# Differential attention: scores of blocks 3 and 4 from stacked rounded and low key halves, and softmax sums folded into the head's norm factor

## The chip, the cores and the metric

The kernel runs on one core of a Trainium2 chip. The metric is device microseconds per execution, lower is better. The kernel as it stands takes 2959.73 us (median of three runs, 2958.84 to 2962.85).

## The reference, cut to what matters

Two layers, each a mixer and a PEER channel mixer, on 512 tokens of width 1024 in float32. The mixer of a layer concatenates three parts (differential attention, short gated convolution, gated linear attention, GLA for short), multiplies by `w_out` and adds to `x`. The change touches the first part alone:

```
def block(args):                       # one of four blocks of 128 queries
    s = jnp.einsum('bqhmd,bkhmd->bhmqk', qi, k).astype(jnp.float32) * scale
    mask = kpos[None, :] <= qpos[:, None]
    p = jax.nn.softmax(jnp.where(mask, s, -jnp.inf), axis=-1)
    a = p[:, :, 0] - lam * p[:, :, 1]
    return jnp.einsum('bhqk,bkhe->bqhe', a.astype(v.dtype), v)
...
o = rmsnorm(o, gain) * out_scale       # over the 128 values of a head
```

There are four heads, and each has two score maps (m = 0, 1) with 64 dimensions. Since the norm divides each head's row by its own size, a factor common to the whole row drops out of it, but for the small eps.

## The kernel before, in words

The 512 tokens are four blocks `tb` = 0 to 3 of 128 queries; "blocks 3 and 4" are `tb` = 2 and 3. `qT` and `kT` hold queries and keys with the head dimensions on partitions: map 0 of a head on rows 0 to 63, map 1 on rows 64 to 127. Block `tb` looks at `(tb + 1) * 128` keys.

A projection product is float32 split in two: `split` (L84, L85) rounds a tile to float32r on ScalarE (`hi`) and takes the rest on VectorE (`lo`); `mm3` (L79 to L81) makes hi·hi + hi·lo + lo·hi, three float32r matmuls. Scores don't use this. They are plain float32 matmuls (L486), and so that one map can be multiplied with 128 rows, `turned_queries` (L477) copies the queries into `qz`, whose rows of the other map are zero.

For each head, `head_weights` makes two scores (L486), adds the causal mask by a bfloat16 matmul (L487), takes the row maximum (L488 on VectorE), the exponentials with their row sums (L493 on ScalarE), and then on VectorE the reciprocals of both sums (L495), map 1's factor with lambda (L496), map 1 times that factor (L497), and the difference (L498). `diff_attention` transposes this on TensorE (`atr`, L512), copies it to SBUF on ScalarE (`aT`, L514) and multiplies it with the values (`po`, L516). `head_norm` squares the four heads of a block in one ScalarE instruction (`ho`, L524), sums on VectorE (`hss`, L525), takes the reciprocal root and multiplies (L527). `head_out` transposes (`htr`, L535) and splits into `mh` and `ml` (L536, L537).

The rest of the mixer is interleaved with this. After the GLA part come blocks 0 and 1, with slab products `psp` of `w_in` (columns from 2048, 1792 and 1536, the three factors of the convolution) between them. In the slab from 1536, after its first half, stand the weights of two heads of block 2 (`early`); `mch` and `mcl` are the convolution's result. Then `w_out` is loaded in eight chunks of 128 rows: `woraw` (SyncE's queue, two buffers in turn), `woh` (ScalarE cast, L84) and `wol` (VectorE, L85). Chunks come in the order `korder` = 6, 7, 4, 5, 0, 1, 2, 3. `out_proj` (`pso`) uses them in that order for both column halves of a block, so that the second pair of products can end only when chunk 3 is there. Two PSUM buffers hold `pso`, two hold `po`, `atr` and `htr`, four hold scores.

The instructions of each engine run in the order in which the building framework's scheduler put them: it keeps program order where data demands it, and otherwise interleaves by its own estimate of times. The placement of tiles in SBUF follows the pools: a pool that is closed gives its memory to the next one opened on that side, and the first writer of such a tile waits for the last readers of what lay there.

Of the kernel before, what the change touches and what calls it, by code (L numbers as in the profile page):

```python
# [7 lines left out]
F32 = mybir.dt.float32  # L8
F32R = mybir.dt.float32r
# [5 lines left out]
OP = mybir.AluOpType  # L15
# [48 lines left out]
def bc(ap, pattern):  # L64
    return bass.AP(tensor=ap.tensor, offset=ap.offset, ap=[ap.ap[0]] + pattern)


class K:
# [152 lines left out]
    def mixer(self, L):  # L221
# [3 lines left out]
        with ExitStack() as mc:  # L225
            mp = mc.enter_context(tc.tile_pool(name="mix", bufs=1, reuse_waits="tile"))
            dgain = mp.tile([P, 1], F32, name="dgain")
            cw = mp.tile([P, 2, 3], F32, name="cw")
            qT = mp.tile([P, 4, T], F32, name="qT")
            kT = mp.tile([P, 4, T], F32, name="kT")  # L230
            va = mp.tile([P, TB, T], F32, name="va")
            if L == 0:
# [5 lines left out]
            with ExitStack() as wc:  # L238
                wp = wc.enter_context(tc.tile_pool(name="wpool", bufs=2, reuse_waits="tile"))
# [75 lines left out]
                lam = mp.tile([P, 1], F32, name="lam")  # L315
                nc.vector.tensor_tensor(lam, le[:, 0:1], le[:, 1:2], op=OP.subtract)
                nc.vector.tensor_scalar(lam, lam, lam_init, None, op0=OP.add)
                nc.vector.tensor_scalar(dgain, dgain, 1.0 - lam_init, None, op0=OP.mult)
# [47 lines left out]
                ap = ac.enter_context(tc.tile_pool(name="attn", bufs=2, side="right", reuse_waits="tile"))  # L366
                qz = [ap.tile([P, 4, 2, P], F32, name=f"qz{i}", bufs=1) for i in range(2)]
                for t in qz:
                    nc.gpsimd.memset(t, 0.0)
                heads = []  # L370

                def attend(tb, early=()):
                    heads.append(self.diff_attention(tb, qT, kT, va, qz[tb % 2], lam, ap, early))

                attend(0)
# [17 lines left out]
                for j, ps in across(1536):  # L393
                    if j == 0:
                        self.turned_queries(2, qT, qz[0])
                        early = [self.head_weights(2, h, kT, qz[0], lam, ap) for h in range(2)]
                    nc.vector.tensor_tensor(ys[j], ys[j], ps, op=OP.mult)
                    self.split(mch[:, j], mcl[:, j], ys[j])

            with tc.tile_pool(name="wout", bufs=1, reuse_waits="tile") as op_:  # L400
# [31 lines left out]
                for tb in range(TB):  # L432
                    if tb > 1:
                        attend(tb, early if tb == 2 else ())
                    t = slice(tb * P, tb * P + P)
                    self.head_out(heads[tb], dgain, mh[:, 0:4, t], ml[:, 0:4, t])
# [35 lines left out]

    def turned_queries(self, tb, qT, qz):
        s = slice(tb * P, tb * P + P)
        for m in range(2):
            r = slice(64 * m, 64 * m + 64)
            self.nc.scalar.copy(qz[r, :, m], qT[r, :, s])  # L477

    def head_weights(self, tb, h, kT, qz, lam, ap):
        nc = self.nc  # L480
        nk = (tb + 1) * P
        st = self.sm.tile([P, 8], F32, tag="st", name="st")
        pss = []
        for m in range(2):
            ps = self.psA.tile([P, T], F32, tag="a", name="pss")
            nc.tensor.matmul(ps[:, 0:nk], qz[:, h, m], kT[:, h, 0:nk], start=True, stop=False)  # L486
            nc.tensor.matmul(ps[:, tb * P:nk], self.identb, self.causal, start=False, stop=True)  # L487
            nc.vector.tensor_reduce(st[:, m:m + 1], ps[:, 0:nk], axis=AX.X, op=OP.max)  # L488
            pss.append(ps)
        nc.vector.tensor_scalar(st[:, 2:4], st[:, 0:2], -0.125, None, op0=OP.mult)  # L490
        e = ap.tile([P, 2, T], F32, tag="e", name="e")
        for m in range(2):
            nc.scalar.activation(e[:, m, 0:nk], pss[m][:, 0:nk], AF.Exp, bias=st[:, 2 + m:3 + m],  # L493
                                 scale=0.125, accum_out=st[:, 4 + m:5 + m])
        nc.vector.reciprocal(st[:, 6:8], st[:, 4:6])  # L495
        nc.vector.tensor_tensor(st[:, 7:8], st[:, 7:8], lam, op=OP.mult)  # L496
        nc.vector.tensor_scalar(e[:, 1, 0:nk], e[:, 1, 0:nk], st[:, 7:8], None, op0=OP.mult)  # L497
# [4 lines left out]
    def diff_attention(self, tb, qT, kT, va, qz, lam, ap, early=()):  # L502
        nc = self.nc
        early = list(early)
        if not early:
            self.turned_queries(tb, qT, qz)
        po = self.psB.tile([P, 4, P], F32, tag="b", name="po")
        for h in range(4):
            e = early.pop(0) if early else self.head_weights(tb, h, kT, qz, lam, ap)
            tr = self.psB.tile([P, 4, P], F32, tag="b", name="atr")  # L510
            for kb in range(tb + 1):
                nc.tensor.transpose(tr[:, kb], e[:, 0, kb * P:kb * P + P], self.ident)  # L512
            aT = ap.tile([P, 4, P], F32, tag="aT", name="aT")
            nc.scalar.copy(aT[:, 0:tb + 1], tr[:, 0:tb + 1])  # L514
            for kb in range(tb + 1):
                nc.tensor.matmul(po[:, h], aT[:, kb], va[:, kb, h * P:h * P + P],  # L516
                                 start=(kb == 0), stop=(kb == tb))
        return self.head_norm(po, 4, P, ap)

    def head_norm(self, po, nh, hd, pool):  # L520
# [3 lines left out]
        nc.scalar.activation(o, po, AF.Square)  # L524
        nc.vector.tensor_reduce(ss, o, axis=AX.X, op=OP.add)  # L525
# [756 lines left out]
```

## Time and profile before

| what | value |
|---|---|
| median of three runs | 2959.73 us (2958.84 to 2962.85) |
| profiled execution, its own time | 2958.37 us |
| its span, first to last instruction | 2956.6 us |
| TensorE busy | 2925.6 us (99%) |
| VectorE busy | 2394.7 us (81%) |
| ScalarE busy | 1256.3 us (42%) |
| granted TensorE clock | 0.999 |
| score matmuls L486 (both layers) | 128 instructions, two for each score |

The stretch that the change touches is 146 to 240 us in the first layer, and the same stretch some 1467.7 us later in the second. In a timeline a row gives start, duration, engine, line, operation, output and inputs, partitions and elements, and the number of instructions merged. Matmuls are pipelined: one's duration is longer than its step, so the price of one is read as the distance between the starts of two. A float32 matmul stands as two instructions.

### The profile page before, as it was taken

To read this page: it belongs to the slowest core of one execution; us is meant where nothing else is said; L and a number is where in the kernel's file an instruction comes from. 1 tells how busy PE (TensorE), PEld (TensorE's weight loads), DVE (VectorE), ACT (ScalarE), POOL (GpSimd) and SP (SyncE) were. 2 spreads that over 40 slices of the span, in tenths; PEclk is the share of its full clock that TensorE was granted. 3 is DMA by queue.
4 is the path that set the end of the run, shared out by engine and by line. 5 is a ranking of instruction groups with operands and counts; after the bars stand their busy time and mean duration, and the time that the engine had idled before them with its cause. 6 is when DMAs were issued, how large, how long until landed. Compare 5 with 4: busy or idle time off the path is not lost.

```text
span 2956.6 us, 44538 instructions
## 1 busy us (share of the span) xinstructions
PE 2925.6 (99%) x16262; PEld 2606.0 (88%) x16262; DVE 2394.7 (81%) x4754; ACT 1256.3 (42%) x1860; POOL 716.0 (24%) x617
## 2 busy tenths in 40 slices
PE   8999999999999999999999999999999999999998
PEld 7878899999999999888888788999999999988887
DVE  6676999976887788877866769999768787888778
ACT  6253355665333332333453433556653333333333
POOL 1200000222444455222012000012225444452220
PEclk9999999999999999999999999999999999999999
DMA  4322257999999998999633222679999999989995
GB/s 130 92 72 77 93 172 250 321 301 362 348 338 326 330 346 310 368 333 342 251 96 90 67 82 86 205 253 330 303 351 356 333 337 332 332 316 358 346 347 203
DMA packets 335835, 760.24 MB, mean 257 GB/s; under 512 B 30688, under 2 KB 191360, under 8 KB 331520
## 3 DMA queue, kind: packets, MB, share of 16 engines
q1 hardware_dynamic: 160624, 435.19, 41.4%
q0 software_dynamic: 75776, 271.62, 26.0%
q10 hardware_dynamic: 99216, 50.60, 5.7%
q8 instruction: 127, 2.08, 0.3%
q14 instruction: 92, 0.75, 0.1%
HBM read 673.15 MB, written 81.00 MB: 255 GB/s over the span
## 4 chain that ended last, share of the span: by engine, by line
PE 84%; DVE 11%; ACT 2%; issue 2%; DMA 1%; SPq 0%; DVEq 0%; ACTq 0%
PE pv L80 11%; PE pv L81 11%; PE pv L79 11%; PE psh L79 9%; PE psh L81 9%; PE psh L80 9%; PE psp L80 2%; PE psp L81 2%; PE psp L79 2%; PE psq L80 2%; PE psq L79 2%; PE psq L81 2%; PE pss L486 1%; PE psg L1211 1%; PE pss L764 1%
## 5 line engine op out<-in xcount | busy, mean ns | idle before, releaser
L827 POOL DMA_INDIRECT row<-in_u_rows,idx x256 | 349.1, 1363 | 1337.6 <-DVE row L834 627.8
L80 PE MATMUL pv<-vl,wh 128*128 128x512 f32 x1500 | 583.9, 389 | 0.4 <-DVE vl L931 0.3
L81 PE MATMUL pv<-vh,wl 128*128 128x512 f32 x1500 | 583.4, 389 | 0.0
L79 PE MATMUL pv<-vh,wh 128*128 128x512 f32 x1500 | 583.2, 389 | 0.0
L827 POOL DMA_INDIRECT row<-in_v_rows,idx x256 | 315.7, 1233 | 597.0 <-DVE yacc L843 548.2
L745 ACT ACTIVATE ht<-psh 128x384 f32<-128x384 f32 x256 | 125.7, 491 | 742.1 <-PE psh L81 741.9
L931 DVE TENSOR_TENSOR vl<-vraw,vh 128x1024 fp32r<-128x1024 f32 x250 | 305.9, 1224 | 115.2 <-ACT vh L936 104.2
L79 PE MATMUL psh<-ahi,uwb 128*128 128x384 f32 x1024 | 346.9, 339 | 0.0
L79 PE MATMUL psh<-ahi,uwa 128*128 128x384 f32 x1024 | 346.4, 338 | 0.0
L81 PE MATMUL psh<-ahi,uwa 128*128 128x384 f32 x1024 | 344.6, 337 | 0.7 <-DVE uwa L730 0.7
L80 PE MATMUL psh<-alo,uwa 128*128 128x384 f32 x1024 | 344.3, 336 | 0.0
L80 PE MATMUL psh<-alo,uwb 128*128 128x384 f32 x1024 | 344.2, 336 | 0.0
L81 PE MATMUL psh<-ahi,uwb 128*128 128x384 f32 x1024 | 344.1, 336 | 0.0
L81 PEld LDWEIGHTS pv<-vh,wl 128*128 128x128 f32 x1500 | 281.4, 188 | 59.6 <-DVE wl L931 1.0
L80 PEld LDWEIGHTS pv<-vl,wh 128*128 128x128 f32 x1500 | 281.4, 188 | 56.6 <-DVE vl L931 2.2
L79 PEld LDWEIGHTS pv<-vh,wh 128*128 128x128 f32 x1500 | 281.6, 188 | 53.9
L843 DVE SCALAR_TENSOR_TENSOR yacc<-row,wk,yacc 128x1024 f32<-128x1024 f32 x254 | 325.2, 1280 | 1.7
L944 ACT CAST wh<-ht 128x384 fp32r<-128x384 f32 x250 | 127.9, 512 | 433.6 <-DVE ht L1096 417.0
L834 DVE SCALAR_TENSOR_TENSOR row<-row,xg 128x1024 f32<-128x1024 f32 x256 | 308.0, 1219 | 0.0
L730 DVE TENSOR_TENSOR uwa<-uraw,uwa 128x1024 fp32r<-128x1024 f32 x144 | 175.7, 1223 | 134.7 <-ACT uwa L729 134.5
L936 ACT CAST vh<-vraw 128x1024 fp32r<-128x1024 f32 x250 | 262.6, 1050 | 9.7 <-DMA vraw<-in_v_rows 9.7
L730 DVE TENSOR_TENSOR uwb<-uraw,uwb 128x1024 fp32r<-128x1024 f32 x144 | 175.8, 1222 | 105.9 <-ACT uwb L729 105.9
(361 smaller groups left out, 5708.6 us busy)
## 6 DMA issues: line engine op xcount, KB each, us to landing
uraw<-in_peer_u SPq DMA_DIRECT2D x256, 512.0 KB, 5.6
vraw<-in_v_rows SPq DMA_DIRECT2D x256, 512.0 KB, 6.5
G<-stg ACTq DMA_DIRECT2D x48, 1024.0 KB, 7.6
g<-G SPq DMA_DIRECT2D x32, 1536.0 KB, 10.0
H<-ht SPq DMA_DIRECT2D x144, 192.0 KB, 4.7
ht<-H SPq DMA_DIRECT2D x144, 192.0 KB, 6.5
wraw<-in_w_in SPq DMA_DIRECT2D x84, 256.0 KB, 3.2
uraw<-in_peer_w_q SPq DMA_DIRECT2D x32, 512.0 KB, 3.5
```

The lines of the kernel that those rows point to most:

```text
L79: mm(ps, ah, bh, start=first, stop=False)
L80: mm(ps, ah, bl, start=False, stop=False)
L81: mm(ps, al, bh, start=False, stop=last)
L486: nc.tensor.matmul(ps[:, 0:nk], qz[:, h, m], kT[:, h, 0:nk], start=True, stop=False)
L730: self.last = pin(nc.vector.tensor_tensor(lo, src, hi.bitcast(F32), op=OP.subtract))
L745: pin(nc.scalar.activation(hs[c], ps, AF.Gelu))
L827: nc.gpsimd.indirect_dma_start(out=r, out_offset=None, in_=ins[name], in_offset=bass.IndirectOffsetOnAxis(ap=idx[:, k:k + 1], axis=0))
L834: nc.vector.scalar_tensor_tensor(r, r, 1.0, xg, op0=OP.mult, op1=OP.mult, accum_out=hd[:, k:k + 1])
L843: nc.vector.scalar_tensor_tensor(yacc, r, wk[:, k:k + 1], yacc, op0=OP.mult, op1=OP.add)
L931: self.last = pin(nc.vector.tensor_tensor(lo, src, hi.bitcast(F32), op=OP.subtract))
L936: pin(nc.scalar.copy(vh[c], vs[c]))
L944: pin(nc.scalar.copy(wh[c], hs[c]))
```

## The change

Scores of blocks 2 and 3 are made from float32r halves. `ks[m]` holds the rounded keys of map m on that map's own 64 rows and their low parts on the other 64, brought there by a GpSimd DMA. `qa` holds the rounded queries of a map on both halves of the rows (the second copy by DMA too), `qb` the low queries. A score is then two float32r matmuls: `qa` with all 128 rows of `ks[m]` (hi·hi + hi·lo), and `qb` with the 64 rows of rounded keys (lo·hi). Keys are stacked block by block (`stack_keys`) behind the slab products, and queries of block 2 and 3 likewise (`stack_queries`); blocks 0 and 1 keep the padded float32 queries.

The weights of a head are no longer normalised by map 0's sum: map 1 is multiplied by -lambda times the ratio of the two sums and added to map 0, which leaves out the instruction on L497. Map 0's sums go into `s0`; `head_norm` takes their reciprocals, squares each head with that scale (four ScalarE instructions with row sums, in place of one and the VectorE sum on L525), and multiplies the norm's factor by it. `lam` changes its sign.

`qT` and `kT` move into a pool that closes with the slabs' pools, so that the first tiles of the `w_out` pool lie where they were.

```
+            raw_qk = wc.enter_context(tc.tile_pool(name="rawqk", bufs=1, reuse_waits="tile"))
+            qT = raw_qk.tile([P, 4, T], F32, name="qT")
+            kT = raw_qk.tile([P, 4, T], F32, name="kT")
...
+                ks = [ap.tile([P, 4, T], F32R, name=f"ks{i}", bufs=1) for i in range(2)]
+                kl = wc.enter_context(tc.tile_pool(name="klow", bufs=2, side="right", reuse_waits="tile"))
...
+                def stack_keys(tb):
+                    t = slice(tb * P, tb * P + P)
+                    lo = kl.tile([P, 4, P], F32R, tag="klo", name="klo")
+                    for m in range(2):
+                        r = half[m]
+                        self.split(ks[m][r, :, t], lo[r], kT[r, :, t])
+                        nc.gpsimd.dma_start(ks[m][half[1 - m], :, t], lo[r])
...
+                def stack_queries(tb):
+                    qa = ap.tile([P, 2, 4, P], F32R, tag="qa", name="qa")
+                    qb = ap.tile([P, 4, P], F32R, tag="qb", name="qb")
+                    for m in range(2):
+                        r = half[m]
+                        self.split(qa[r, m], qb[r], qT[r, :, tb * P:tb * P + P])
+                        nc.gpsimd.dma_start(qa[half[1 - m], m], qa[r, m])
+
+                    def stacked(ps, h, m, nk):
+                        nc.tensor.matmul(ps, qa[:, m, h], ks[m][:, h, 0:nk], start=True, stop=False)
+                        nc.tensor.matmul(ps, qb[half[m], h], ks[m][half[m], h, 0:nk], start=False, stop=False)
+                    return stacked
...
                 for j, ps in across(2048):
                     nc.scalar.copy(z[:, j, 2:], ps)
-                attend(1)
+                    stack_keys(j)
+                attend(1, padded_queries(1))
                 for j, ps in across(1792):
                     nc.vector.tensor_tensor(z[:, j, 2:], ps, z[:, j, 2:], op=OP.mult)
+                    if j:
+                        score2 = stack_queries(2)
+                    else:
+                        stack_keys(2)
...
                     if j == 0:
-                        self.turned_queries(2, qT, qz[0])
-                        early = [self.head_weights(2, h, kT, qz[0], lam, ap) for h in range(2)]
+                        s0 = self.sums()
+                        early = [s0] + [self.head_weights(2, h, score2, lam, ap, s0) for h in range(2)]
+                        stack_keys(3)
+                        score3 = stack_queries(3)
...
-            nc.tensor.matmul(ps[:, 0:nk], qz[:, h, m], kT[:, h, 0:nk], start=True, stop=False)
+            score(ps[:, 0:nk], h, m, nk)
...
-        nc.vector.reciprocal(st[:, 6:8], st[:, 4:6])
-        nc.vector.tensor_tensor(st[:, 7:8], st[:, 7:8], lam, op=OP.mult)
-        nc.vector.tensor_scalar(e[:, 1, 0:nk], e[:, 1, 0:nk], st[:, 7:8], None, op0=OP.mult)
-        nc.vector.scalar_tensor_tensor(e[:, 0, 0:nk], e[:, 0, 0:nk], st[:, 6:7], e[:, 1, 0:nk],
-                                       op0=OP.mult, op1=OP.subtract)
+        nc.vector.reciprocal(st[:, 4:5], st[:, 4:5])
+        nc.vector.scalar_tensor_tensor(st[:, 5:6], st[:, 4:5], lam, s0[:, h:h + 1], op0=OP.mult, op1=OP.mult)
+        nc.vector.scalar_tensor_tensor(e[:, 0, 0:nk], e[:, 1, 0:nk], st[:, 5:6], e[:, 0, 0:nk],
+                                       op0=OP.mult, op1=OP.add)
...
-        nc.scalar.activation(o, po, AF.Square)
-        nc.vector.tensor_reduce(ss, o, axis=AX.X, op=OP.add)
+        nc.vector.reciprocal(s0, s0)
+        for h in range(nh):
+            nc.scalar.activation(o[:, h], po[:, h], AF.Square, scale=s0[:, h:h + 1], accum_out=ss[:, h:h + 1])
         rstd = self.rsqrt(ss, hd)
+        nc.vector.tensor_tensor(rstd, rstd, s0, op=OP.mult)
         nc.vector.tensor_tensor(o, po, bc(rstd, [[1, nh], [0, hd]]), op=OP.mult)
```

ScalarE in block 0 of the first layer, before. `e` are exponentials, `qz` the padded queries, `aT` the transposed weights, `ho` the squares.

```order
L477 COPY qz_1504<-qT 64x4x128 x2
L84 CAST wh<-wraw 128x512
L493 ACTIVATE e,st<-pss,st 128x128 x4
L477 COPY qz_1503<-qT 64x4x128 x2
L514 COPY aT<-atr 128x128
L493 ACTIVATE e,st<-pss,st 128x128 x2
L379 COPY z<-psp 128x512
```

The same engine, the end of block 0 after the change (lines are the changed file's).

```order
L526 ACTIVATE e,st<-pss,st 128x128
L84 CAST ks_1506<-kT 64x4x128
L545 COPY aT<-atr 128x128
L84 CAST ks_1507<-kT 64x4x128
L84 CAST qa<-qT 64x512
L545 COPY aT<-atr 128x128
L84 CAST qa<-qT 64x512
L84 CAST ks_1506<-kT 64x4x128
L560 ACTIVATE ho,hss<-po,s_1517 128x128 x4
```

Casts of keys and queries now stand between the copies `aT` for which TensorE's `po` waits, and all casts of blocks 0 to 3 stand ahead of the slab from 1536.

TensorE where block 2's last heads give way to block 3's scores, before. `mgh` is GLA's result in `out_proj`.

```order
L512 MATMUL atr<-ident,e 128x128 x3
L486 MATMUL pss<-kT,qz_1504 128x512
L487 LDWEIGHTS identb
L487 MATMUL pss<-causal,identb 128x128
L486 MATMUL pss<-kT,qz_1504 128x512
L516 MATMUL po<-va,aT 128x128 x3
```

The same place after the change.

```order
L543 MATMUL atr<-ident,e 128x128 x3
L393 MATMUL pss<-ks_1506,qa 128x512
L394 MATMUL pss<-ks_1506,qb 128x512
L520 LDWEIGHTS identb
L520 MATMUL pss<-causal,identb 128x128
L393 MATMUL pss<-ks_1507,qa 128x512
L394 MATMUL pss<-ks_1507,qb 128x512
```

A score is two matmuls in place of one, of 128 and of 64 rows, with the mask behind them as before.

TensorE around the last chunk of `w_out`, before; the last row but one is the first that reads chunk 3.

```order
L535 MATMUL htr<-ident,ho 128x128 x4
L512 MATMUL atr<-ident,e 128x128 x4
L80 MATMUL pso<-wol,mh 128x512
L81 MATMUL pso<-woh,ml 128x512
L79 MATMUL pso<-woh,mh 128x512 x2
L516 MATMUL po<-va,aT 128x128 x4
```

And after the change, where the last row is the first that reads chunk 3.

```order
L571 MATMUL htr<-ident,ho 128x128 x4
L543 MATMUL atr<-ident,e 128x128 x4
L79 MATMUL pso<-woh,mh 128x512 x2
L547 MATMUL po<-va,aT 128x128 x4
L543 MATMUL atr<-ident,e 128x128 x4
L80 MATMUL pso<-wol,mh 128x512
L81 MATMUL pso<-woh,ml 128x512
L79 MATMUL pso<-woh,mh 128x512
```

One head's `po` and the next head's `atr` of block 3 moved ahead of the first use of chunk 3.

More of the change, by code (lines that the diff above doesn't have):

```diff
@@ L228, in mixer @@
             cw = mp.tile([P, 2, 3], F32, name="cw")
-            qT = mp.tile([P, 4, T], F32, name="qT")
-            kT = mp.tile([P, 4, T], F32, name="kT")
             va = mp.tile([P, TB, T], F32, name="va")
+            wc = mc.enter_context(ExitStack())
+            raw_qk = wc.enter_context(tc.tile_pool(name="rawqk", bufs=1, reuse_waits="tile"))
+            qT = raw_qk.tile([P, 4, T], F32, name="qT")
+            kT = raw_qk.tile([P, 4, T], F32, name="kT")
             if L == 0:
@@ L237, in mixer @@
                 hh, hl = self.hh, self.hl
-            with ExitStack() as wc:
+            with wc:
                 wp = wc.enter_context(tc.tile_pool(name="wpool", bufs=2, reuse_waits="tile"))
@@ L366, in mixer @@
                 ap = ac.enter_context(tc.tile_pool(name="attn", bufs=2, side="right", reuse_waits="tile"))
-                qz = [ap.tile([P, 4, 2, P], F32, name=f"qz{i}", bufs=1) for i in range(2)]
+                ks = [ap.tile([P, 4, T], F32R, name=f"ks{i}", bufs=1) for i in range(2)]
+                kl = wc.enter_context(tc.tile_pool(name="klow", bufs=2, side="right", reuse_waits="tile"))
+                qz = [kl.tile([P, 4, 2, P], F32, name=f"qz{i}", bufs=1) for i in range(2)]
                 for t in qz:
@@ L369, in mixer @@
                     nc.gpsimd.memset(t, 0.0)
+                half = [slice(64 * m, 64 * m + 64) for m in range(2)]
+                def stack_keys(tb):
[5 more added lines that the diff above has]
+                        nc.gpsimd.dma_start(ks[m][half[1 - m], :, t], lo[r])
@@ L370, in mixer, with padded_queries, attend @@
+                def padded_queries(tb):
+                    for m in range(2):
+                        nc.scalar.copy(qz[tb][half[m], :, m], qT[half[m], :, tb * P:tb * P + P])
+                    return lambda ps, h, m, nk: nc.tensor.matmul(ps, qz[tb][:, h, m], kT[:, h, 0:nk], start=True, stop=False)
                 heads = []
-                def attend(tb, early=()):
-                    heads.append(self.diff_attention(tb, qT, kT, va, qz[tb % 2], lam, ap, early))
-                attend(0)
+                def attend(tb, score, early=()):
+                    heads.append(self.diff_attention(tb, score, va, lam, ap, early))
@@ L433, in mixer @@
                     if tb > 1:
-                        attend(tb, early if tb == 2 else ())
+                        attend(tb, *((score2, early) if tb == 2 else (score3,)))
                     t = slice(tb * P, tb * P + P)
@@ L471, in rope, with head_weights @@
                 nc.gpsimd.dma_start(dst[64 * m:64 * m + 16, 2 * h:2 * h + 2], rot[32 * h + 16 * m:32 * h + 16 * m + 16])
[L473 to L479, printed above, removed]
+    def head_weights(self, tb, h, score, lam, ap, s0):
         nc = self.nc
         nk = (tb + 1) * P
-        st = self.sm.tile([P, 8], F32, tag="st", name="st")
+        st = self.sm.tile([P, 6], F32, tag="st", name="st")
         pss = []
@@ L493, in head_weights, with diff_attention @@
             nc.scalar.activation(e[:, m, 0:nk], pss[m][:, 0:nk], AF.Exp, bias=st[:, 2 + m:3 + m],
-                                 scale=0.125, accum_out=st[:, 4 + m:5 + m])
-        nc.vector.reciprocal(st[:, 6:8], st[:, 4:6])
-        nc.vector.tensor_tensor(st[:, 7:8], st[:, 7:8], lam, op=OP.mult)
-        nc.vector.tensor_scalar(e[:, 1, 0:nk], e[:, 1, 0:nk], st[:, 7:8], None, op0=OP.mult)
-        nc.vector.scalar_tensor_tensor(e[:, 0, 0:nk], e[:, 0, 0:nk], st[:, 6:7], e[:, 1, 0:nk],
-                                       op0=OP.mult, op1=OP.subtract)
+                                 scale=0.125, accum_out=st[:, 4:5] if m else s0[:, h:h + 1])
+        nc.vector.reciprocal(st[:, 4:5], st[:, 4:5])
+        nc.vector.scalar_tensor_tensor(st[:, 5:6], st[:, 4:5], lam, s0[:, h:h + 1], op0=OP.mult, op1=OP.mult)
+        nc.vector.scalar_tensor_tensor(e[:, 0, 0:nk], e[:, 1, 0:nk], st[:, 5:6], e[:, 0, 0:nk],
+                                       op0=OP.mult, op1=OP.add)
         return e
-    def diff_attention(self, tb, qT, kT, va, qz, lam, ap, early=()):
+    def diff_attention(self, tb, score, va, lam, ap, early=()):
         nc = self.nc
         early = list(early)
-        if not early:
-            self.turned_queries(tb, qT, qz)
+        s0 = early.pop(0) if early else self.sums()
         po = self.psB.tile([P, 4, P], F32, tag="b", name="po")
         for h in range(4):
-            e = early.pop(0) if early else self.head_weights(tb, h, kT, qz, lam, ap)
+            e = early.pop(0) if early else self.head_weights(tb, h, score, lam, ap, s0)
             tr = self.psB.tile([P, 4, P], F32, tag="b", name="atr")
@@ L517, in diff_attention, with sums, head_norm @@
                                  start=(kb == 0), stop=(kb == tb))
-        return self.head_norm(po, 4, P, ap)
-    def head_norm(self, po, nh, hd, pool):
+        return self.head_norm(po, 4, P, ap, s0)
+    def sums(self):
+        return self.sm.tile([P, 4], F32, tag="s0", name="s0")
+    def head_norm(self, po, nh, hd, pool, s0):
         nc = self.nc
```

5 lines of the change are left out of this document (3 added, 2 removed).

## The prediction

> **What bounds the kernel now.** I read the page first, then the waits and the windows of the attention stretch, then its timelines.
>
> ```profile
> span 2956.6 us, 44538 instructions
> PE 2925.6 (99%) x16262; PEld 2606.0 (88%) x16262; DVE 2394.7 (81%) x4754; ACT 1256.3 (42%) x1860; POOL 716.0 (24%) x617
> PE 84%; DVE 11%; ACT 2%; issue 2%; DMA 1%; SPq 0%; DVEq 0%; ACTq 0%
> ```
>
> TensorE is busy for 99% of the span and holds 84% of the chain that ended last: what comes off its work comes off the time, as long as something else is ready. Whether something is ready must be read in the stretch itself. The windows of the first layer cover blocks 0 and 1 (150 to 178) and the end of the attention with the `w_out` load (197 to 224); columns are length, then busy time of TensorE, weight loads, VectorE, ScalarE and GpSimd.
>
> ```profile
> 150.00:162.00 12.00, 11.86 (x67) 8.74 (x66) 7.18 (x31) 8.81 (x29) 0.00 (x0) 1.00 0.31 89
> 162.00:178.00 16.00, 16.00 (x85) 12.10 (x84) 13.45 (x46) 9.99 (x29) 0.00 (x0) 1.00 0.06 17
> 197.00:212.00 15.00, 14.38 (x72) 8.90 (x71) 13.49 (x29) 10.55 (x23) 0.00 (x0) 1.00 0.22 71
> 212.00:224.00 12.00, 12.00 (x56) 8.39 (x55) 11.18 (x29) 6.32 (x12) 0.00 (x0) 1.00 0.50 175
> ```
>
> From 197 to 224 VectorE is busy 24.67 of 27 us, nearly as full as TensorE. The waits from 186 to 245 (sum, times, longest) say what else runs at its limit there.
>
> ```profile
> ACT woh L84 <- DMA woraw<-in_w_out: 4.5, 4, 2.3
> PEld po L516 <- ACT aT L514: 2.7, 8, 0.9
> PEld pso L79 <- ACT woh L84: 0.9, 2, 0.5
> ```
>
> ScalarE waits 4.5 us for `w_out`, and TensorE already waits a little for ScalarE's chunks. With two buffers a chunk can be loaded only when VectorE has finished the one two places before it. ScalarE's casts 1, 4, 6 and 8 of the eight:
>
> ```profile
> 202.58 1.05 ACT L84 CAST woh<-woraw 128x1024 fp32r<-128x1024 f32 x1
> ...
> 211.01 1.04 ACT L84 CAST woh<-woraw 128x1024 fp32r<-128x1024 f32 x1 [0.30 <-DMA woraw<-in_w_out]
> ...
> 217.25 1.05 ACT L84 CAST woh<-woraw 128x1024 fp32r<-128x1024 f32 x1 [1.63 <-DMA woraw<-in_w_out]
> ...
> 223.68 1.04 ACT L84 CAST woh<-woraw 128x1024 fp32r<-128x1024 f32 x1
> ```
>
> The even casts follow each other by 6.24 and 6.43 us: a chain of load, cast and subtraction that no shorter matmul speeds up. Chunk 3 (cast 8) is a gate: the first block's output products can't end before it, and all others come behind them. So work taken from TensorE ahead of the gate pays only if other work fills the place.
>
> **The score itself.** Scores of block 2 (384 keys) and of block 3 (512 keys) on TensorE:
>
> ```profile
> 187.94 0.81 PE L486 MATMUL pss<-kT,qz 128*128 128x384 f32 x2
> 188.58 0.22 PE L487 MATMUL pss<-causal,identb 128*128 128x128 bf16 x1
> 188.64 0.86 PE L486 MATMUL pss<-kT,qz 128*128 128x384 f32 x2
> ...
> 190.88 0.48 PE L79 MATMUL psp<-ahi,wh 128*128 128x512 f32 x1
> 191.19 0.40 PE L80 MATMUL psp<-alo,wh 128*128 128x512 f32 x1
> 191.43 0.39 PE L81 MATMUL psp<-ahi,wl 128*128 128x512 f32 x1
> ...
> 213.26 1.03 PE L486 MATMUL pss<-kT,qz 128*128 128x512 f32 x2
> ...
> 215.12 0.48 PE L81 MATMUL pso<-woh,mcl 128*128 128x512 f32 x1
> ```
>
> Four scores with masks take 187.94 to 190.88, 0.735 us each; two of block 3 take 213.26 to 215.12, 0.93 each. A float32r matmul of 512 columns steps by about 0.23 (191.19 to 191.43 is 0.24), so one of 384 is estimated at three quarters, 0.17; the first one behind a mask takes 0.31, 0.08 more; the mask steps 0.06. The new score is then 0.17 + 0.17 + 0.08 + 0.06 = 0.48 for 384 keys and 0.23 + 0.23 + 0.14 = 0.60 for 512. It saves 0.255 and 0.33; with eight of each, 4.7 us in a layer, 9.4 in both.
>
> The second matmul has 64 rows, between two instructions of 128. GLA has such ones (`psu`, float32), and they are dear:
>
> ```profile
> 87.97 1.99 PE L610 MATMUL pst<-qs,ks 128*128 128x256 f32 x8
> 89.90 0.70 PE L648 MATMUL psu<-gv,kdT 64*128 64x256 f32 x2
> 90.52 1.13 PE L610 MATMUL pst<-qs,ks 128*128 128x256 f32 x4
> ```
>
> ```profile
> 1542.37 0.70 PE L648 MATMUL psu<-gv,kdT 64*128 64x256 f32 x2 [0.36 <-DVE S L650]
> 1542.99 0.51 PE L80 MATMUL psp<-alo,wh 128*128 128x512 f32 x1
> ...
> 1543.57 0.40 PE L79 MATMUL psp<-ahi,wh 128*128 128x512 f32 x1
> ```
>
> Four matmuls of 128 rows and 256 columns take 1.93, 0.48 each; the one of 64 rows and as many columns takes 0.62, so 0.14 more. Between float32r matmuls it takes 1.20 to the start of the third row, less two steps of 0.23 that is 0.74, so 0.26 more. The excursion to 64 rows costs 0.14 to 0.26 a score by these rows, perhaps nothing and perhaps more for a float32r one; I take 0.20, between the two. A score then saves 0.055 and 0.13: 8 × 0.055 + 8 × 0.13 = 1.5 us a layer. At 0.14 it is 2.4, at 0.26 some 0.5.
>
> By the Trainium skill (TensorE: Matmul & The Clock Gate, Step-by-step: what each phase is for) the number of rows doesn't matter to a weight load and the streaming takes one cycle a column, which would make the excursion free and the term 4.7. By its page TensorEngine Tiling (Array Packing), Key Properties, changing the tiling mode, not just the tile, drains TensorE, and this speaks against the change; the `psu` rows agree with the second page.
>
> **What of it is on the path.** Four scores stand between the slab's halves, where TensorE is full: 4 × 0.055 = 0.2 off. Everything up to the first cast of `w_out` moves with it. The other twelve, 4 × 0.055 + 8 × 0.13 = 1.3, stand ahead of the gate. The order puts a `po` and an `atr` of block 3 ahead of chunk 3:
>
> ```profile
> 225.51 0.90 PE po L516 x8
> 226.41 0.44 PE atr L512 x4
> ```
>
> That is 1.3 us of filler, just enough. The gate itself moves by the 0.2, and by little more: VectorE loses L497 and `hss` here (below), but the load chain has only some tenths to give. I take 1.35 of the 1.5 as gained.
>
> **Stacking, blocks 0 and 1.** Rows of the nearest kind: the query copies, a VectorE subtraction of 512 columns, and a GpSimd DMA's bytes and time to landing.
>
> ```profile
> L477 ACT COPY qz<-qT x16: 616/619/627, 149.6 to 1638.2; 64x512 f32<-64x512 f32 x16
> ```
>
> ```profile
> 189.51 0.69 DVE L85 TENSOR_TENSOR mcl<-y,mch 128x512 fp32r<-128x512 f32 x1
> 203.20 0.42 DVE L497 TENSOR_SCALAR e<-e,st 128x384 f32<-128x384 f32 x1
> 214.30 0.69 DVE L525 TENSOR_REDUCE hss<-ho 128x4 f32<-128x512 f32 x1 [0.32 <-ACT ho L524]
> ```
>
> ```profile
> qT<-rot POOLq DMA_DIRECT2D x4, 64.0 KB, 2.5
> ```
>
> ScalarE gets 12 casts of 0.62 (7.4 us) and loses four copies (2.5); VectorE gets 12 subtractions of 0.69 (8.3) and loses eight L497 here, each 0.42 at most, and two `hss`: about 4.5 net. All of it is ordered into 150 to 178, where ScalarE is busy 18.8 and VectorE 20.6 of 28 us: they go to about 25 each with `ho` below. What hides it is the slab products, of which the order keeps 43 rows ahead of block 2's scores (some 10 us). But TensorE's `po` waits for `aT`, and casts of 0.62 now stand before some of them. It can gain up to 0.5 (a shorter VectorE chain for each head) and lose up to 3 (five casts that stand between the `aT`); I take 0.5 lost. The DMAs are ten on an idle GpSimd; at 2.5 us, or twice that for the larger ones, they land by about 175, ahead of 187.94: nothing, and a microsecond for each that came late. SyncE's order is unchanged, and the first `w_out` loads wait for the queries' casts, which come before the slab's end: nothing.
>
> **Head norm.** One `ho` becomes four instructions with row sums; those of the exponentials step by 0.36.
>
> ```profile
> 153.10 0.36 ACT L493 ACTIVATE e<-pss,st 128x128 f32<-128x128 f32 x1
> 153.46 0.36 ACT L493 ACTIVATE e<-pss,st 128x128 f32<-128x128 f32 x1
> 213.66 0.60 ACT L524 ACTIVATE ho<-po 128x512 f32<-128x512 f32 x1
> ```
>
> Four are 1.4 against 0.60 + 0.69 for `ho` and `hss`: about even, and a small multiplication more. For block 3 `htr` waits for it behind 18 output products; I take 0.2 lost.
>
> **The sum.** A layer: -1.35 + 0.5 + 0.2 = -0.65. Two layers: -1.3, against the profiled execution's 2958.37 (span 2956.6 and 1.8 around it). That execution lies 1.4 below the median of 2959.73, so the forecast on the median is 2958.4. About 0.2% (5.9 us) is what a measurement of this kernel can tell from no change.
>
> **The rivals.** *The excursion is free* (the first page's rule). For it: these are float32r, not the two-pass float32 of `psu`. Against it: both `psu` rows. Then 4.7 a layer leaves TensorE, and 0.7 is lost to stacking and norm: 8.0 in both layers, 2951.7, if filler is found at the gate. If the gate keeps what its 1.3 of filler doesn't cover (4 × 0.255 + 8 × 0.33 = 3.7 stand ahead of it), 2.4 a layer are lost again and it is 2956.5. Chance 0.22, of which I give the first case a little over half.
>
> *The excursion costs more than the passes save.* A 64-row weight load that can't be brought forward beside a 128-row matmul, twice a score, on TensorE's own path. From about 0.3 on the scores save nothing; at 0.45 they lose 8 × 0.195 + 8 × 0.12 = 2.5 a layer, with stacking and norm 3.2, and the time is 2966.1. For it: 0.26 was for one excursion among float32r. Against it: that row's F32 matmul loads weights twice, the new one once. The page on tiling is the rule in question here. Chance 0.11.
>
> *Stacking fills ScalarE and VectorE in blocks 0 and 1* so that every head's `aT` is late: 3 lost there instead of 0.5, a layer 1.85 slower, 2963.4. For it: both engines reach 25 of 28 us. Against it: the slab products. Chance 0.12.
>
> The forecast has 0.55; its own range is 2955 to 2961.
>
> **Range and chances.** The range takes in the free excursion and the filled engines, and leaves out most of the dear one: 2951.5 to 2964.0. Faster by over 0.2% (below 2953.8): the first rival without the gate, 0.13, and the forecast's edge, 0.02. Slower by over 0.2% (above 2965.6): 0.07 of the second rival, 0.02 of the third and 0.03 for what I have not seen. The rest is within.
>
> **What would show it.** In the changed profile: the step from one score of block 2 to the next (forecast 0.68, 0.48 if free) and of block 3 (0.80, 0.60); the even casts of `woh` still 6.2 to 6.5 apart; TensorE's waits for `aT` in 150 to 178 up by about 0.5; `htr` of block 3 waiting some tenths longer. The prediction is wrong if a score step falls outside 0.6 to 0.75 for 384 keys, or if block 2's scores start more than 2 us later or earlier than 187.94.

## The result and the profile after

| | before | after |
|---|---|---|
| median of the runs, us | 2961.29 (2958.84 to 2963.61, 4 runs) | 3002.88 (3000.07 to 3004.34, 4 runs) |
| profiled execution, us | 2958.37 | 3004.34 |
| its span, us | 2956.6 | 3002.6 |
| mean granted clock | 0.999 | 0.996 |

The changed kernel is slower: ratio 1.0144, with a 95% interval of 1.0131 to 1.0156, so about 42 us. The forecast was 2958.4, with a range up to 2964.0. One execution each of two experiments below (the shifts by 64 and by 256 bytes) ran at a mean granted clock of 0.75 and 0.81 and took 3617.70 and 3366.72 us; these two are left out of the medians. The page of after, in the lines that answer to the first ones of before:

```profile
span 3002.6 us, 44700 instructions
PE 2962.5 (99%) x16262; PEld 2631.6 (88%) x16262; DVE 2396.2 (80%) x4754; ACT 1269.0 (42%) x1932; POOL 725.9 (24%) x641
PE 91%; DVE 3%; ACT 2%; DMA 2%; issue 1%; SPq 0%; ACTq 0%; DVEq 0%
```

TensorE has as many matmuls as before, 16262, and is busy 36.9 us longer: the loss isn't waiting alone, its matmuls themselves take longer. Where, is seen when the same instruction is looked up in both traces (starts in us):

| instruction | before | after | later by |
|---|---|---|---|
| block 2's first score, layer 1 | 187.94 | 188.52 | 0.6 |
| PEER's first query product (`psq`) | 268.80 | 275.61 | 6.8 |
| first `psh` (PEER's first products) | 375.1 | 383.1 | 8.0 |
| first `pv` (PEER's second products) | 741.09 | 754.63 | 13.5 |
| last `psh` of layer 1 | 1170.64 | 1192.04 | 21.4 |
| last `pv` of layer 1 | 1485.20 | 1506.17 | 21.0 |
| block 2's first score, layer 2 | 1655.62 | 1678.22 | 22.6 |
| first `psq`, layer 2 | 1736.81 | 1767.26 | 30.5 |
| last `psh`, layer 2 | 2637.61 | 2683.12 | 45.5 |
| last `pv`, layer 2 | 2948.27 | 2993.77 | 45.5 |

There are two kinds of places. From block 2's first score to PEER's first product the layers lose 6.2 and 7.9 us: this is the changed stretch. From there to the last `psh` they lose 14.6 and 15.0 us, in a stage where no instruction was changed. Only the stretches of `pv` alone, behind the last `psh`, lose nothing.

**The stage that wasn't changed.** A row of `psh` matmuls on TensorE before, its first and last:

```profile
735.72 0.34 PE L81 MATMUL psh<-ahi,uwb 128*128 128x384 f32 x1
...
740.92 0.34 PE L81 MATMUL psh<-ahi,uwb 128*128 128x384 f32 x1
```

And one after:

```profile
747.80 0.34 PE L80 MATMUL psh<-alo,uwb 128*128 128x384 f32 x1
...
752.57 0.34 PE L80 MATMUL psh<-alo,uwb 128*128 128x384 f32 x1
```

30 steps take 5.20 us before, 173.3 ns each, 27 steps 4.77 after, 176.7 each. The busy time of one, 0.34, hardly shows it: of pipelined matmuls the step from start to start is to be read. A layer has 3072 `psh`, and 3072 × 3.3 ns is 10 us. The `pv` that stand among `psh` step slower too, by 229.0 ns in place of 226.8, which is 2 us a layer. What is left of the 14.6 and 15.0 us is mostly waiting. TensorE stops where before it didn't, behind the first `psq` (0.76 us, shown below) and at the first `pv`, here in layer 1:

```profile
754.63 0.50 PE L79 MATMUL pv<-vh,wh 128*128 128x512 f32 x1 [1.55 <-ACT vh L972]
755.89 0.60 PE L80 MATMUL pv<-vl,wh 128*128 128x512 f32 x1 [0.76 <-DVE vl L967]
```

In layer 2 the two stops at `pv` are 0.63 and 0.76 us. Behind each pair the clock is halved for 3.4 us, which loses 1.7.

**The changed stretch.** The windows that answer to those of before, with the granted clock in the third column from the end:

```profile
150.00:162.00 12.00, 12.00 (x69) 9.14 (x68) 10.99 (x36) 11.78 (x35) 3.12 (x6) 1.00 0.62 133
162.00:178.00 16.00, 15.70 (x83) 11.41 (x81) 14.40 (x48) 12.03 (x38) 3.90 (x7) 1.00 0.49 88
...
197.00:212.00 15.00, 13.56 (x65) 8.85 (x64) 10.55 (x22) 8.17 (x19) 0.00 (x0) 0.89 0.16 45
212.00:224.00 12.00, 11.06 (x50) 7.32 (x49) 10.07 (x26) 7.85 (x19) 0.00 (x0) 1.00 0.36 123
```

VectorE does less from 197 to 224 than before (20.6 us for 24.7), not more: it waits. TensorE is busy 1.8 us less there, and from 197 to 212 it had 0.89 of its clock. The waits of after from 186 to 290:

```profile
ACT woh L84 <- DMA woraw<-in_w_out: 5.5, 3, 3.3
ACT uwa L765 <- PE pso L80: 5.4, 1, 5.4
DVE st L521 <- PE pss L520: 4.1, 6, 1.3
PEld pso L80 <- DVE wol L85: 2.1, 2, 1.4
```

The last three have no row among the first twenty of before. The even casts of `woh` on ScalarE after (2, 4, 6 and 8):

```profile
205.52 1.05 ACT L84 CAST woh<-woraw 128x1024 fp32r<-128x1024 f32 x1
...
214.60 1.06 ACT L84 CAST woh<-woraw 128x1024 fp32r<-128x1024 f32 x1
...
221.75 1.04 ACT L84 CAST woh<-woraw 128x1024 fp32r<-128x1024 f32 x1 [1.45 <-DMA woraw<-in_w_out]
...
228.96 1.05 ACT L84 CAST woh<-woraw 128x1024 fp32r<-128x1024 f32 x1 [0.76 <-DMA woraw<-in_w_out]
```

Their steps are 9.08, 7.15 and 7.21 us, where the last two were 6.24 and 6.43 before. The scores themselves, of 384 keys and then of 512:

```profile
188.52 0.34 PE L393 MATMUL pss<-ks,qa 128*128 128x384 f32 x1
188.79 0.43 PE L394 MATMUL pss<-ks,qb 64*128 64x384 f32 x1
189.16 0.23 PE L520 MATMUL pss<-causal,identb 128*128 128x128 bf16 x1
189.19 0.42 PE L393 MATMUL pss<-ks,qa 128*128 128x384 f32 x1
...
190.71 0.42 PE L393 MATMUL pss<-ks,qa 128*128 128x384 f32 x1
...
214.00 0.47 PE L393 MATMUL pss<-ks,qa 128*128 128x512 f32 x1
214.41 0.50 PE L394 MATMUL pss<-ks,qb 64*128 64x512 f32 x1
214.84 0.23 PE L520 MATMUL pss<-causal,identb 128*128 128x128 bf16 x1
214.87 0.48 PE L80 MATMUL pso<-wol,mgh 128*128 128x512 f32 x1
```

A score of 384 keys behind another one steps by 0.76 (two steps from 189.19 to 190.71), as before (188.64 to 189.39 is 0.75), and one of 512 by 0.87 (214.00 to 214.87), where it took 0.92 (213.26 to 214.18). The first of a row has no mask just ahead of it and is shorter, 0.67 here and 0.70 before (187.94 to 188.64).

### The profile page after: what moved, and what is told of

Same layout as the page of the kernel before. It is cut to its first block, busy times and chain, and to the rows that moved or that the text cites. A ratio compares the mean times of both kernels' runs of the same rounds, so it can differ in the third digit from the quotient of the medians.

```text
span 3002.6 us, 44700 instructions
## 1 busy us (share of the span) xinstructions
PE 2962.5 (99%) x16262; PEld 2631.6 (88%) x16262; DVE 2396.2 (80%) x4754; ACT 1269.0 (42%) x1932; POOL 725.9 (24%) x641
## 4 chain that ended last, share of the span: by engine, by line
PE 91%; DVE 3%; ACT 2%; DMA 2%; issue 1%; SPq 0%; ACTq 0%; DVEq 0%
PE psh L79 12%; PE psh L80 12%; PE psh L81 12%; PE pv L80 11%; PE pv L81 11%; PE pv L79 11%; PE psp L80 2%; PE psp L81 2%; PE psp L79 2%; PE psq L79 2%; PE psq L80 2%; PE psq L81 2%; PE psg L1247 1%; PE psg L1248 1%; PE pss L800 1%
## 5 line engine op out<-in xcount | busy, mean ns | idle before, releaser
L863 POOL DMA_INDIRECT row<-in_v_rows,idx x256 | 307.8, 1202 | 610.9 <-DVE yacc L879 563.0
```

What stands on the lines that cost most here:

```text
L863: nc.gpsimd.indirect_dma_start(out=r, out_offset=None, in_=ins[name], in_offset=bass.IndirectOffsetOnAxis(ap=idx[:, k:k + 1], axis=0))
```

## The experiments

Each was timed in 5 rounds (the shifts by 64 and 192 bytes in 3) beside the kernel before on the same chip; before's medians beside them were 2960.78 (first to fourth), 2960.74 (fifth to eighth), 2960.25 (ninth to eleventh) and 2959.99 us (twelfth). They are told here by subject; the expectations number them as they ran: first and second the 128 bytes added and taken away, third softmax and norm, fourth all 128 rows, fifth `w_out`'s tiles moved, sixth to eighth shifts by 256, 64 and 192, ninth a tile for each chunk, tenth and eleventh `htr`'s buffer, twelfth 64 rows again.

**A place in SBUF.** The new tile `s0` (four buffers of 16 bytes, padded to 32) moves all that lies behind the small pool by 128 bytes, PEER's weights too (by the allocation `uwa` begins at 80672 in place of 80544). The first two experiments put that in alone, and take it out alone.

```
 before, in setup:
+        nc.vector.memset(self.sm.tile([P, 4], F32, tag="s0", name="s0"), 0.0)
```

> The kernel before, with four unused buffers of 32 bytes added to the pool of small tiles. Every instruction and its order are those of before (one 4-column memset more); every tile behind that pool lies 128 bytes further, as in the changed kernel. Theory A, that the place of the weights in SBUF makes the changed kernel's matmuls slower: PEER's psh steps go from 173 to about 176 ns as after the change, psp from 229 to 233 and from 113 to 118, and the time is about 2961 + 26 = 2987 us (6144 psh x 3.0 ns = 18.5, about 1050 psp x 4 = 4.2, the rest from pv). Rival B, that the steps are slower because of what the new instructions do (GpSimd's DMAs, TensorE's use of 64 rows, the clock): steps as before and 2961 us.

```
 the changed kernel:
-        return self.sm.tile([P, 4], F32, tag="s0", name="s0")
+        return self.sm.tile([P, 4], F32, tag="s0", name="s0", bufs=2)
-        ss = self.sm.tile([P, nh], F32, tag="hss", name="hss")
+        ss = self.sm.tile([P, nh], F32, tag="hss", name="hss", bufs=2)
```

> The changed kernel, with two buffers in place of four for the new sums and for the head norm's sums, so that both together take the place that the head norm's alone took. PEER's tiles and the slabs' weights lie where they lay before; the order of instructions is that of the changed kernel on every engine. Theory A: psh steps back to 173 ns, psp to 229 and 113, about 26 us less: 2977 us; what is left over the kernel before, about 16, is the two attention stretches and the four dips of the granted clock. Rival B: 3003 us, steps as after the change.

Measured: 2983.55 us with the 128 bytes added to before (ratio 1.0075, 1.0061 to 1.0089), 2977.69 with them taken from the changed kernel (1.0054, 1.0040 to 1.0067). That is 22.8 more and 25.2 less, against 26 by theory A and nothing by rival B. `psh` of before with the 128 bytes, on TensorE:

```profile
737.69 0.34 PE L80 MATMUL psh<-alo,uwb 128*128 128x384 f32 x1
...
745.64 0.34 PE L80 MATMUL psh<-alo,uwb 128*128 128x384 f32 x1
```

and of the changed kernel without them:

```profile
737.80 0.34 PE L81 MATMUL psh<-ahi,uwa 128*128 128x384 f32 x1
...
746.64 0.34 PE L81 MATMUL psh<-ahi,uwb 128*128 128x384 f32 x1
```

45 steps in 7.95 us are 176.7 ns, 51 steps in 8.84 are 173.3. The place alone does it, in either kernel; B is out. The first experiment's trace keeps the full clock until its last 8 us, so no dip is in its 22.8 us.

Three more shifts, by the number of buffers of that tile (8 in the changed kernel, 2 and 6 in before):

```
+        nc.vector.memset(self.sm.tile([P, 4], F32, tag="s0", name="s0", bufs=2), 0.0)
```

> The changed kernel with eight buffers of the new sums in place of four: everything behind the pool lies another 128 bytes further, 256 in all from before. Order as in the changed kernel. Theory A1, that a place counts by its remainder in 256 bytes: psh back to 173 ns, 2977.7 us as in the second run. Rival A2, that it is a matter of distance or of which tiles lie near each other, so that further is worse or the same: 3003 us or more.

> The kernel before with 64 bytes more in the small pool. If a matmul's step grows evenly with the shift, half of the first run's loss: psh about 174.5 ns, 2972 us. If the place counts in blocks of 128 bytes, tiles that began at 32 within a block of 128 now begin at 96 and reach into the next: any of 2961 (no loss), 2984 (all of it) tells which.

> The kernel before with 192 bytes more in the small pool. With a period of 256 this is 64 bytes back: by the even theory as at 64, about 2972 us; if it is a distance that counts, more than at 128: 2990 us or more. A time under 2961 would say that before did not lie at the best place.

The mean step from one matmul to the next of the same tile, in ns (the longer steps where a group begins are left out), by how far the weights lie behind their place in before:

| shift | kernel | `psh`, 384 columns | `psp`, 512 | `psp`, 256 | time, us |
|---|---|---|---|---|---|
| 0 | before | 173.4 | 229.3 | 113.4 | 2960.74 |
| 64 | before | 173.4 | 227.7 | 120.0 | 2969.88 |
| 128 | before | 176.6 | 233.3 | 117.8 | 2983.55 |
| 192 | before | 175.0 | 232.4 | 119.3 | 2975.77 |
| 0 | changed | 173.4 | 229.9 | 113.5 | 2977.69 |
| 128 | changed | 176.6 | 233.3 | 117.8 | 3002.88 |
| 256 | changed | 173.4 | 229.3 | 113.4 | 2979.96 |

A1 holds: at 256 the steps are those of before at 0 to a tenth of a nanosecond (of the changed kernel at 0 to 0.6). The loss doesn't grow evenly with the shift, and each kind of matmul has its own best place; with 64 bytes `psh` loses nothing and `psp` of 256 columns most. Of the four places before had the best. The 9 us at 64 bytes are mostly not in these columns: `pv` among `psh` steps by 229.2 ns there, and at layer 1's first `pv` TensorE stops for 1.88 and 0.76 us, with the clock halved behind it. And a place doesn't slow every matmul that reads a shifted tile: PEER's query products of 512 columns (`psq`), which read the same `uwa` and `uwb`, step by 233.1 ns in before and 233.3 with the 128 bytes.

**Softmax and norm alone**, on the kernel before (the parts of the change in `head_weights`, `lam` and `head_norm`, with two buffers for `s0` and `hss`):

```
-        nc.vector.tensor_scalar(e[:, 1, 0:nk], e[:, 1, 0:nk], st[:, 7:8], None, op0=OP.mult)
...
+        nc.vector.scalar_tensor_tensor(st[:, 5:6], st[:, 4:5], lam, s0[:, h:h + 1], op0=OP.mult, op1=OP.mult)
...
+            nc.scalar.activation(o[:, h], po[:, h], AF.Square, scale=s0[:, h:h + 1], accum_out=ss[:, h:h + 1])
```

> The kernel before with the change's softmax and head norm alone (old scores, no stacking, no byte moved behind the small pool). If the softmax and norm cost nothing, as the prediction had it: 2959 to 2962 us, even casts of woh 6.2 to 6.5 us apart. Rival: the new order that they give VectorE and ScalarE is what stretches the chain of w_out's chunks (casts 1 to 8 take 25 us in the changed kernel, 21 before): 4 us a layer, 2969 us.

2958.34 us (0.9993, 0.9984 to 1.0002), and the even casts of `woh` are 6.94, 5.71 and 6.32 us apart (201.70, 208.64, 214.35 and 220.67). The rival is out: this part doesn't stretch the chain.

**The 64 rows**, on the second experiment's kernel:

```
-                        nc.tensor.matmul(ps, qb[half[m], h], ks[m][half[m], h, 0:nk], start=False, stop=False)
+                        nc.tensor.matmul(ps, qb[:, h], ks[m][:, h, 0:nk], start=False, stop=False)
```

> The changed kernel at the old addresses (as the second kernel of this call), with the score's second matmul on all 128 rows in place of 64: it adds the product of the other map's low query half with the low keys to each score. Order as there. If a turn to 64 rows and back is what eats the saving: score step for 384 keys from 0.755 to about 0.48, for 512 from 0.87 to 0.60, 16 x 0.27 = 4.3 us a layer less on TensorE, so 6 to 9 us under the second kernel's time if it is on the path. Rival: the stretch waits for ScalarE, VectorE and w_out, and the time is within 2 us of the second kernel's.

2970.49 us (1.0032, 1.0020 to 1.0043), 7.2 below the second experiment, as the theory had it. TensorE, the scores between the slab's halves and the second half of block 2:

```profile
187.55 0.42 PE L393 MATMUL pss<-ks,qa 128*128 128x384 f32 x1
187.81 0.34 PE L394 MATMUL pss<-ks,qb 128*128 128x384 f32 x1
187.99 0.23 PE L520 MATMUL pss<-causal,identb 128*128 128x128 bf16 x1
188.03 0.42 PE L393 MATMUL pss<-ks,qa 128*128 128x384 f32 x1
```

```profile
197.23 0.23 PE L520 MATMUL pss<-causal,identb 128*128 128x128 bf16 x1
198.95 0.52 PE L543 MATMUL atr<-ident,e 128*128 128x128 f32 x3 [1.49 <-DVE ml L573]
200.09 1.24 PE L547 MATMUL po<-va,aT 128*128 128x128 f32 x6 [0.62 <-ACT aT L545]
```

With all rows a score steps by 0.48, with 64 by 0.76: the turn to 64 rows and back costs 0.28 us. But TensorE, now earlier, stops for 1.49 us in the same place where the changed kernel stops for 0.65: `atr` needs the PSUM buffer that VectorE's `ml` still reads. The changed kernel there:

```profile
201.84 0.52 PE L543 MATMUL atr<-ident,e 128*128 128x128 f32 x3 [0.65 <-DVE ml L573]
```

**PEER's first weights.** The changed kernel, ScalarE and then TensorE at the end of layer 1's mixer:

```profile
274.51 1.99 ACT L765 CAST uwa<-uraw 128x1024 fp32r<-128x1024 f32 x2 [5.37 <-PE pso L80]
```

```profile
275.61 0.39 PE L79 MATMUL psq<-ahi,uwa 128*128 128x256 f32 x1 [0.91 <-ACT uwa L765]
...
276.86 0.39 PE L81 MATMUL psq<-ahi,uwa 128*128 128x256 f32 x1 [0.76 <-DVE uwa L766]
```

Since `qT` and `kT` are freed ahead of the `w_out` load, `mh` lies where PEER's first `uwa` goes (85184 to 93376 and 80672 to 88864); before, `kT` and `va` lay there, long read. The first attempt moved tiles:

```
-                mh = op_.tile([P, 4, T], F32R, name="mh")
-                ml = op_.tile([P, 4, T], F32R, name="ml")
                 wh = op_.tile([P, KD, D], F32R, name="woh")
                 wl = op_.tile([P, KD, D], F32R, name="wol")
+                mh = op_.tile([P, 4, T], F32R, name="mh")
+                ml = op_.tile([P, 4, T], F32R, name="ml")
...
-                    self.split(wh[:, k], wl[:, k], raw)
+                    i = korder.index(k)
+                    self.split(wh[:, i], wl[:, i], raw)
...
```

> The kernel of the fourth run (128 rows in the score's second matmul, addresses of PEER and slabs as before) with w_out's tiles placed anew: the halves of w_out stand ahead of mh and ml and in the order in which the output products use them. No order changes. In that run and in the changed kernel TensorE stops for 0.91 and 0.76 us at PEER's first query products (271 us) and the granted clock then halves for 3.41 us: PEER's first uwa lies on mh, which the last output products still read; before it lay on kT and va. Theory: both stops and the dip go in both layers, 2 x (0.91 + 0.76 + 1.7) = 6.7 us: 2970.5 - 6.7 = 2963.8. Rival: the cast of uwa waits for its load or for ScalarE, and the time stays within 1.5 us of 2970.5.

2969.18 us (1.0026, 1.0016 to 1.0037): no change. (The halved clock that the expectation speaks of stands behind these stops in the second and the fourth experiment's traces, at 274 and 272 us; in the changed kernel's trace the clock stays full there.) The cast waited as long:

```profile
269.75 1.99 ACT L766 CAST uwa<-uraw 128x1024 fp32r<-128x1024 f32 x2 [5.61 <-PE pso L81]
```

The rival's number, but not its cause: the wait still ends with the last output product. All eight chunks were one tile, and it counts as read until its last reader. So the next made tiles of them:

```
-                wh = op_.tile([P, KD, D], F32R, name="woh")
-                wl = op_.tile([P, KD, D], F32R, name="wol")
+                wh = {k: op_.tile([P, D], F32R, name=f"woh{k}") for k in korder}
+                wl = {k: op_.tile([P, D], F32R, name=f"wol{k}") for k in korder}
...
```

> The fifth run (128 rows, w_out's halves ahead of mh and ml) with each of the eight chunks of both halves a tile of its own; the order is that of the fourth and fifth. There the first cast of uwa waited 5.4 to 5.6 us for the last output product, because the whole of mh, and in the fifth the whole of w_out's half, was one tile that is free only after its last reader. Theory: with a chunk as a tile the cast waits only for the chunk under it, the stops of 0.91 and 0.76 us at PEER's first query products and the dip of the clock there go in both layers: 2970.5 - 6.7 = 2963.8. Rival: something else holds the cast and the time stays within 1.5 us of 2970.

2961.95 us (1.0007, 0.9998 to 1.0017), 8.5 below the fourth experiment and 7.2 below the fifth. ScalarE's cast there:

```profile
264.94 1.05 ACT L765 CAST uwa<-uraw 128x1024 fp32r<-128x1024 f32 x1 [0.76 <-PE pso L81]
```

TensorE goes from `pso` to `psq` without a stop, in both layers.

**The stop ahead of block 2's second half.**

```
-                    self.head_out(heads[tb], dgain, mh[:, 0:4, t], ml[:, 0:4, t])
+                    self.head_out(heads[tb], dgain, mh[:, 0:4, t], ml[:, 0:4, t], self.psC if tb < 2 else self.psB)
...
```

> The kernel of the run before it in this call, with the transposes htr of blocks 0 and 1 in the PSUM buffers of the products (psC) in place of the two that po and atr use. In the fourth run TensorE stops for 1.49 us ahead of block 2's second half: atr needs the buffer that VectorE's ml still reads, behind three maxima of scores; the clock halves in the first layer. Theory: stop and dip go, 1.5 to 3.2 us a layer, 2963.8 - 4.5 = 2959. Rival: the stop moves to the next thing that is late there (aT, w_out's chunks), and the time stays within 1.5 us of the run before it.

> The third run (the kernel before with the new softmax and head norm) with htr of blocks 0 and 1 in psC. There atr waits 0.2 to 0.6 us at the same place and the clock does not dip: theory, 0 to 1 us a layer less, 2957.5, the fastest so far. Rival: the new order of the output products puts them ahead of work that w_out's chain needs, and it is slower than 2958.3.

The tenth takes 2956.10 us (0.9989, 0.9980 to 0.9998): the fastest, and the first that is below before by more than its interval. The windows of 197 to 224 are without a dip, and VectorE is full again:

```profile
197.00:212.00 15.00, 14.49 (x87) 10.68 (x86) 13.81 (x31) 12.06 (x26) 0.00 (x0) 1.00 0.32 107
212.00:224.00 12.00, 10.64 (x54) 7.23 (x52) 10.71 (x26) 8.01 (x19) 0.00 (x0) 1.00 0.42 131
```

Scores of 512 keys with all rows, in the tenth:

```profile
202.08 0.50 PE L393 MATMUL pss<-ks,qa 128*128 128x512 f32 x1 [0.26 <-ACT e L526]
...
202.69 0.48 PE L393 MATMUL pss<-ks,qa 128*128 128x512 f32 x1
```

They step by 0.61. The eleventh takes 2958.21 us (0.9995, 0.9986 to 1.0004), as without its edit: in the third `atr` comes only 0.21 us behind the last mask, so next to nothing was to be had, and neither theory can be told from the other.

**The change with all this mended**, 64 rows again in the tenth's kernel:

> The kernel of the tenth run with the score's second matmul on its 64 rows again, as in the change: all that the change does, with the addresses, w_out's tiles and htr mended. In the tenth run a score of 384 keys steps by 0.474 us and one of 512 by 0.61; in the second, with 64 rows, by 0.755 and 0.87. Theory, that what TensorE spends here is on the path once the stops are gone: 8 x 0.28 + 8 x 0.26 = 4.3 us a layer, 2956.1 + 8.6 = 2964.7. Rival, that the chain of w_out's chunks holds the end of the stretch, so that only the four scores between the slab's halves count (1.1 us a layer): 2958.3.

2961.05 us (1.0004, 0.9995 to 1.0013), 5 above the tenth, between the two numbers: by the medians a little over half of what 64 rows cost TensorE is on the path, and the two intervals are too wide to say it closer. The change's own idea, with nothing else spoilt, leaves the time as it was.

So the 46.8 us between the changed kernel and the tenth, removed one after the other: the place in SBUF 25.2 (3002.88 to 2977.69), the 64 rows 7.2, the tile under `uwa` 8.5, `htr`'s buffer 5.9. Another order of removal would share them out differently: the 64 rows came to 7.2 here and to 5 in the twelfth. Each share holds the dips of the clock that went with it.

## Why the prediction was wrong

**The step that failed most is the one that wasn't there.** "The sum" was made of terms of one stretch and took the rest of the program to move along with it. 25.2 of the 41.6 us come from PEER and the slabs, by the 128 bytes; the forecast had nothing for them. The diff shows `s0` in the small pool, ahead of every pool that is opened later; the prediction looked at orders, durations and waits, and not at places, and it had no row to price such a shift.

**"SyncE's order is unchanged ... nothing" and the moved tiles.** It looked at what the freed `qT` and `kT` let the `w_out` load do, and not at what then lies under the next stage's first tile. That cost TensorE two stops in each layer, 0.91 and 0.76 us, and in some traces a dip of the clock behind them. A tile for each chunk took 8.5 us off.

**The excursion.** Taken at 0.20 us, with 0.14 and 0.26 as bounds; measured 0.28 for 384 keys (0.76 less 0.48) and 0.26 for 512 (0.87 less 0.61). The mechanism was right and the size too small. The step for a score, forecast at 0.68 and 0.80, is 0.76 and 0.87. Whether its own condition for being wrong (outside 0.6 to 0.75 for 384 keys) is met hangs on the reading: 0.76 between two scores is outside, but the forecast started from the mean of four with their first, 0.735, and that mean is now 0.74 (188.52 to 191.47), inside. So scores of 384 keys save nothing and those of 512 about 0.05 each, some 0.4 us a layer where the forecast had 1.5: this alone is 2 us of the miss. The free score was estimated well: 0.48 and 0.60 for a measured 0.48 and 0.61. The Trainium skill (TensorEngine Tiling (Array Packing), Key Properties) says that a change of mode drains TensorE, and the 0.28 us agree with it, though no run shows what the time goes into. The rival that the rows are free is out.

**"The gate itself moves by the 0.2, and by little more."** It moved by 5.3 us (last cast 223.68 to 228.96), and the even casts, forecast to stay 6.2 to 6.5 apart, are 7.15 and 7.21 apart. The chain of load, cast and subtraction isn't one of fixed steps: its casts and subtractions stand in order behind exponentials and maxima that wait for scores, and the scores behind `atr`, which waited 0.65 to 1.49 us for a buffer. VectorE reads three maxima ahead of `ml` now, two before. Moving `htr` to another buffer, and no cheaper instruction, brought 5.9 us, and in the tenth the last cast is at 221.86.

**What held.** Stacking: block 2's first score is 0.6 us later (the prediction's sign of being wrong was 2), VectorE and ScalarE are busy 25.4 and 23.8 of 28 us there (forecast 25), and with the old addresses that score comes 1.4 us earlier than before, at 186.57; the rival that they fill up is out. Head norm and softmax were costed at 0.2 us a layer more and are even or 1.2 less. With the place, the tiles and `htr`'s buffer mended the time is 2961.05, within 0.2% of before, where the forecast put the change itself. This is partly luck, since `htr`'s buffer brought something that the change doesn't have; and the forecast was on the kernel, which is 1.4% slower.

## What to carry to other kernels

Before costing what a change does, compare where its tiles lie: a small tile in a pool that is opened early moves everything behind it, and a freed tile puts others under the first tiles of the next stage. Look at the step between matmuls in stages that the change doesn't touch: here the shifted places cost 25 us, and all else that the change did cost 16. A short stop of TensorE should be priced at its length and the dip of the clock that may follow.

## What the runs showed of the hardware

**The place of a matmul's operands can change its step.** Shifting the weights by 128 bytes, with the other operand where it was, took `psh` from 173.4 to 176.6 ns and `psp` from 229.3 to 233.3 and 113.4 to 117.8; a shift by 256 gave the old steps back. In stretches of `pv` alone, where both operands moved together, nothing was lost (314.1 us after, 314.6 before, in layer 1). The Trainium skill (SBUF — State Buffer, A bandwidth-pool intuition that's wrong) gives weight loads a read port of their own. By that alone these shifts would not be expected to cost anything, and the measurements decide. Why 0 and 256 bytes are alike and the shifts between them not, no run here shows.

**After short stops the clock may halve.** The changed kernel's TensorE around its stops of 0.65 and 0.62 us, with the granted clock third from the end:

```profile
199.78:203.19 3.41, 2.13 (x10) 1.19 (x10) 3.27 (x8) 0.83 (x3) 0.00 (x0) 1.00 0.00 0
203.19:206.59 3.40, 3.40 (x13) 2.44 (x12) 1.08 (x4) 3.25 (x8) 0.00 (x0) 0.50 0.00 0
206.59:210.00 3.41, 3.25 (x19) 2.27 (x19) 2.88 (x3) 1.48 (x5) 0.00 (x0) 1.00 0.19 44
```

A row of 3.4 us in which TensorE was busy 2.13 is followed by one at half clock: 1.7 us lost. In that execution it happened four times (at 203, 756 and 2248 for 3.4 us, at 1691 for 10.2), 10.2 us in all; in the tenth experiment's only at the very end. The Trainium skill (TensorE: Matmul & The Clock Gate, Part 1: The HAM clock gate) gives the length of such a window as 3413 ns, which agrees, and puts an idle window ahead of it; here it took no idle one. How long TensorE is busy in a row doesn't decide it either. The same trace around the stops of 0.91 and 0.76 us, and ahead of the dip at 1691:

```profile
274.87:278.28 3.41, 1.92 (x13) 1.72 (x14) 2.70 (x3) 2.58 (x3) 0.00 (x0) 1.00 0.19 26
278.28:281.69 3.41, 3.41 (x31) 3.41 (x30) 1.76 (x3) 1.44 (x2) 0.00 (x0) 1.00 0.90 302
...
1687.98:1691.39 3.41, 2.90 (x12) 1.45 (x11) 2.75 (x6) 1.58 (x3) 0.00 (x0) 1.00 0.00 0
1691.39:1701.63 10.24, 9.48 (x31) 6.71 (x31) 5.31 (x10) 5.04 (x12) 0.00 (x0) 0.50 0.20 56
```

A row with 1.92 us busy kept the full clock, and one with 2.90 lost it for three rows. What decides stays open, so such a dip can be looked for but not forecast from these runs.
